# Feed-forward of a streaming encoder: up-projection in seven block products, down-projection summed in PSUM

## The chip, the core and the metric

The kernel runs on one core of a Trainium2 chip. The time is the device time of one execution in microseconds. TensorE (PE) does the matrix products into PSUM, VectorE (DVE), ScalarE (ACT) and GpSimd (POOL) the elementwise work, and SyncE (SP) issues most transfers.

## The reference

One layer of an encoder runs over a prompt of 2048 tokens and a sample of 32 (T = 2080, D = 1024). After the mixing sub-layer comes the feed-forward, which the change concerns:

```python
def conv_ffn(h, conv_state, w_up, w_dw, b_dw, w_down):
    t = h.shape[1]
    u = h @ w_up                                  # 1024 -> 2 x 2816
    uu = jnp.concatenate([conv_state.astype(u.dtype), u], axis=1)
    y = b_dw
    for j in range(CONV_W):                       # 3 taps, causal, over time
        y = y + w_dw[j] * uu[:, j:j + t]
    a, g = jnp.split(y, 2, axis=-1)
    out = (jax.nn.gelu(a, approximate=True) * g) @ w_down    # 2816 -> 1024
    return out, uu[:, -(CONV_W - 1):]
...
    h = rmsnorm(x, p['g_pre_ffn']) * (1.0 + scale_f) + shift_f
    yf, conv_new = conv_ffn(h, s_conv, p['w_up'], p['w_dw'], p['b_dw'], p['w_down'])
    x = x + gate_f * rmsnorm(yf, p['g_post_ffn'])
```

## The kernel before

Everything is kept transposed: features on the 128 partitions, tokens along the columns. Each float32 operand of a product is split into a high part (`hi`, rounded by ACT to the matmul's format) and the rest (`lo`, DVE's subtraction); `split` does that, and `mm3` makes a product of three matmuls, hi x hi, hi x lo, lo x hi.

The kernel runs through the input projection, the two mixers, and then blocks of 260 tokens (`merge`, `project`, `norms`) that merge the branches, project, normalise and write the feed-forward's input to `h2T` in DRAM. The generator `norms` of a block is advanced by `step()` while TensorE works on the next block; the last block's runs inside the feed-forward.

The feed-forward takes the tokens in six segments of 348 or 346 columns (`segs`; two more columns of the past are loaded for the conv), two segments (`si`) at a time in three passes (`sb`). `load_seg` brings a segment's eight k tiles in and splits them. For each row tile m of the 2816 (MF = 22) and each segment, `up` makes two products, the a half and the g half (`x` = 0, 1), over eight k tiles into a PSUM bank `px`; ACT and DVE apply the three conv taps, gelu and the product a*g, and split the result into an `ACT` tile. The last segment also holds the place where prompt and sample meet: `conv_outputs` copies the conv state in and the last rows out (L1397 to L1399).

`down` follows after each two row tiles: for the eight output tiles it multiplies two k tiles and adds the bank `po` to an accumulator `acc` in SBUF (L1443, L1445). After the last of them the segment's squares are summed, and `post` normalises, adds x1 and stores. Raw weights come through `wur` and `wdr` and are split by `split_up` and `split_down`, one step ahead.

The order on TensorE is that of the code. On the other engines a scheduler sets the order at build time; each then works through its queue in that order, and a waiting instruction holds those behind it. SP's queue is such a queue for the transfers.

## Time and profile before

| | us |
|---|---|
| median of 3 runs (3396.43 to 3398.52) | 3397.34 |
| the profiled execution, its own time | 3400.56 |
| its span | 3398.8 |
| PE busy | 3291.8 |
| DVE busy | 2037.2 |
| ACT busy | 1399.4 |
| POOL busy | 442.9 |

The span is the time from the first to the last instruction in the trace; the execution's own time has a few microseconds around it. The page gives the busy time of each engine with its number of instructions, then the span in 40 equal slices of about 85 us (each digit is the busy share in tenths; PEclk is TensorE's granted clock in tenths), and groups of equal instructions: line, engine, operation, output<-inputs, shapes, count, then busy time in total and mean ns of one, then idle time of the engine just before them with what ended it. In a view of windows the columns are: window, length, busy time (and count) of PE, of the weight loads, DVE, ACT and POOL, granted clock, share of the DMA engines, GB/s.

### The profile page before, as it was taken

How to read it: one execution, taken by the hardware profiler on the slowest of the kernel's cores; microseconds unless marked ns; L12 is line 12 of the kernel's file. 1: busy time of each engine (PE TensorE's matmuls, PEld its weight loads, DVE VectorE, ACT ScalarE, POOL GpSimd, SP SyncE). 2: the span in 40 equal slices, each digit the busy share in tenths (PEclk: the TensorE clock that was granted, in tenths of full speed). 3: DMA queues.
4: the chain of work that ended last, by engine and by line, in shares of the span. 5: the costliest groups of instructions: out<-in, count | busy, mean ns of one | idle time of the engine just before them, and what ended most of it. 6: DMA issues, size and time to landing. Idle time of an engine off the chain costs nothing. (4 is left out here: it accounts for less than half of the span.)

```text
span 3398.8 us, 56935 instructions
## 1 busy us (share of the span) xinstructions
PE 3291.8 (97%) x21114; PEld 3154.4 (93%) x21114; DVE 2037.2 (60%) x4837; ACT 1399.4 (41%) x3226; POOL 442.9 (13%) x593
## 2 busy tenths in 40 slices
PE   6999999999999999999999999999999999999997
PEld 5899998888999999889999999999999999999997
DVE  6735436673455555665767565557555567666666
ACT  4412224443444555544556433326433336433333
POOL 3102101111111111113544000001000001100001
PEclk8999999999999999999999999999999999999998
DMA  6434434444333334745556322224322224322211
GB/s 211 121 119 136 132 108 125 127 115 134 105 113 108 108 110 132 222 145 165 174 155 201 108 63 75 69 69 130 97 74 71 67 75 121 96 75 66 72 50 52
DMA packets 429319, 381.97 MB, mean 112 GB/s; under 512 B 40529, under 2 KB 396194, under 8 KB 429042
## 3 DMA queue, kind: packets, MB, share of 16 engines
q1 hardware_dynamic: 386082, 332.15, 33.4%
q10 hardware_dynamic: 42704, 45.93, 4.2%
q8 instruction: 166, 2.72, 0.3%
q14 instruction: 111, 0.91, 0.1%
q0 software_dynamic: 256, 0.26, 0.0%
HBM read 280.71 MB, written 97.51 MB: 111 GB/s over the span
## 5 line engine op out<-in xcount | busy, mean ns | idle before, releaser
L76 PE MATMUL px<-hA,hA 128*128 128x350 f32 (+2 forms) x2144 | 692.1, 323 | 0.0
L78 PE MATMUL px<-hA,hA 128*128 128x350 f32 (+2 forms) x2144 | 690.4, 322 | 0.0
L77 PE MATMUL px<-hA,hA 128*128 128x350 f32 (+1 forms) x2112 | 680.0, 322 | 0.0
L76 PEld LDWEIGHTS px<-hA,hA 128*128 128x128 f32 x2144 | 404.3, 189 | 0.1
L78 PEld LDWEIGHTS px<-hA,hA 128*128 128x128 f32 x2144 | 404.2, 189 | 0.0
L77 PEld LDWEIGHTS px<-hA,hA 128*128 128x128 f32 x2112 | 398.7, 189 | 0.0
L76 PE MATMUL po<-mhl,hA 128*128 128x348 f32 (+2 forms) x1184 | 372.1, 314 | 13.4 <-DVE acc L1445 7.4
L77 PE MATMUL po<-mhl,hA 128*128 128x348 f32 (+2 forms) x1184 | 369.9, 312 | 3.9 <-DVE mhl L1207 3.9
L78 PE MATMUL po<-mhl,hA 128*128 128x348 f32 (+2 forms) x1120 | 349.8, 312 | 0.0
L1445 DVE TENSOR_TENSOR acc<-acc,po 128x348 f32<-128x348 f32 (+1 forms) x480 | 242.9, 512 | 132.3 <-PE po L78 131.8
L76 PE MATMUL pm<-hA,wh 128*128 128x416 f32 x768 | 289.3, 377 | 0.0
L1418 DVE SCALAR_TENSOR_TENSOR y<-px,cw,y 128x346 f32<-128x346 f32 (+1 forms) x264 | 152.0, 576 | 215.4 <-ACT y L1417 215.2
L77 PE MATMUL pm<-hA,wh 128*128 128x416 f32 x768 | 270.4, 352 | 0.0
L78 PE MATMUL pm<-hA,wl 128*128 128x416 f32 x768 | 270.0, 352 | 0.0
L1417 ACT ACTIVATE y<-px,cw 128x346 f32<-128x346 f32 (+1 forms) x264 | 166.9, 632 | 228.1 <-PE px L78 214.0
L76 PEld LDWEIGHTS po<-mhl,hA 128*128 128x128 f32 x1184 | 224.8, 190 | 22.2 <-DVE acc L1445 12.3
L77 PEld LDWEIGHTS po<-mhl,hA 128*128 128x128 f32 x1184 | 225.5, 190 | 5.3 <-DVE mhl L1207 5.2
L70 DVE TENSOR_TENSOR hA<-wur,hA 128x1024 fp32r<-128x1024 f32 x132 | 162.8, 1234 | 101.5 <-ACT hA L67 100.0
L78 PEld LDWEIGHTS po<-mhl,hA 128*128 128x128 f32 x1120 | 213.1, 190 | 0.0
L1493 POOL TENSOR_TENSOR acc<-acc,x 128x346 f32<-128x346 f32 (+3 forms) x48 | 48.5, 1019 | 1010.0 <-DVE acc L1489 1001.2
L76 PE MATMUL pn<-wh,hA 128*128 128x256 f32 (+1 forms) x624 | 177.7, 285 | 0.0
L78 PE MATMUL pn<-wh,hA 128*128 128x256 f32 (+1 forms) x624 | 176.9, 284 | 0.0
(353 smaller groups left out, 7648.8 us busy)
## 6 DMA issues: line engine op xcount, KB each, us to landing
wur<-in_w_up_dram SPq DMA_DIRECT2D x132, 512.0 KB, 3.9
wdr<-in_w_down_dram SPq DMA_DIRECT2D x66, 512.0 KB, 4.3
wr<-in_w_in_dram SPq DMA_DIRECT2D x76, 256.0 KB, 3.5
sgT<-tx ACTq DMA_DIRECT2D x80, 208.0 KB, 2.5
wa<-in_w_ada_dram SPq DMA_DIRECT2D x64, 256.0 KB, 3.3
keys<-ks SPq DMA_DIRECT2D x128, 128.0 KB, 2.9
xk<-in_xT_dram SPq DMA_DIRECT2D x20, 416.0 KB, 4.9
tg<-sgT SPq DMA_DIRECT2D x40, 208.0 KB, 2.8
```

The costliest lines, as they stand in the source:

```text
L70: nc.vector.tensor_sub(lo, src, f32(hi))
L76: nc.tensor.matmul(out, ah, bh, start=first and i == 0, stop=False)
L77: nc.tensor.matmul(out, ah, bl, start=False, stop=False)
L78: nc.tensor.matmul(out, al, bh, start=False, stop=last and i == n - 1)
L1417: nc.scalar.activation(y[:, :o], p[:, 2:n], AF.Identity, bias=cw[:, c, 3:4], scale=cw[:, c, 2:3])
L1418: nc.vector.scalar_tensor_tensor(y[:, :o], p[:, 1:n - 1], cw[:, c, 1:2], y[:, :o], op0=OP.mult, op1=OP.add)
L1445: nc.vector.tensor_add(ac[:, m, :o], ac[:, m, :o], p[:, :o])
L1493: add.tensor_add(ac[:, m, a:e], ac[:, m, a:e], x[:, m % 2, a:e])
```

## The change

The up-projection now takes two segments together (a pair p; three pairs). The weights of a row tile are cut into four blocks, a and g half by the first and second four k tiles: A11 and A12 are the a half's, A21 and A22 the g half's. The pair's columns form B likewise (B11, B12 for the first four k tiles of the two segments, B21, B22 for the rest). Instead of eight block products there are seven, of twelve matmuls each: A11 B11, A12 B21, S1 T1, S2 T2, S3 T3, S4 B22, A22 T4, with sums S1 = A21 + A22, S2 = S1 - A11, S3 = A11 - A21, S4 = A12 - S2 of the weights and T1 to T4 of the columns.

- The column sums are made by GpSimd in `sums`, once a pair, and written to `hT` in DRAM; those of pairs 0 and 1 during the blocks of `merge` and `project`, those of pair 2 after the last block's norms, inside the feed-forward. `load_ops` reads and splits the operands of a pair, those of the next pair at the row tiles 14, 16, 18 and 21.
- The weight sums are made by GpSimd in `weights` for every row tile of every pair, into the tiles s0 to s3 (for S1 to S4; one buffer each, raw weights in `wur`). ACT makes the hi parts, DVE the lo parts, but that of A22 is GpSimd's. Split weights go round in a ring of nine places.
- `up` makes the products and joins them: p1 is A11 B11 copied out of PSUM by ACT, P5 is S1 T1, U2 is S2 T2 plus p1 and U3 is S3 T3 on top of that (both DVE). The sum of U3 and P5, the g half of the second segment, is GpSimd's (CG). DVE adds U2 to the a half of the second segment in PSUM. The g half of the first segment (`g_half`, product A22 T4) is made one row tile later, and then YG, the g half's conv, and the product with ya, the gelu. The six conv copies stand in the third pair, for both halves.
- The activations are written unsplit to `actD` in DRAM, and the accumulator, its additions, and the interleaved `down` are gone. After all three pairs the down-projection runs pair by pair and output tile by output tile over all 22 k tiles in one PSUM tile `ad` of two banks (`load_acts` brings a pair's activations back and splits them; the down weights are read again for each pair). `post` works on both segments of a pair at once.

```diff
@@ merge
-            p = psX.tile([128, 512], F32, name="px", tag=f"x{m % 2}")
+            if m % 2 == 0:
+                ad = psX.tile([128, 2, 512], F32, name="ad", tag="ad")
+            p = ad[:, m % 2]
@@ sums of the columns
+    def h_tile():
+        return fp0.tile([128, 2, W], F32, name="ht", tag="ht", bufs=3)
+    def sums(p):
+        w = WP[p]
+        for j in range(4):
+            x, y = h_tile(), h_tile()
+            load_h(x, [(0, j, 2 * p), (1, j, 2 * p + 1)], w)
+            load_h(y, [(0, 4 + j, 2 * p), (1, 4 + j, 2 * p + 1)], w)
+            yield
+            x0, x1, y0, y1 = x[:, 0, :w], x[:, 1, :w], y[:, 0, :w], y[:, 1, :w]
+            nc.gpsimd.tensor_sub(x0, x1, x0)
+            nc.gpsimd.tensor_sub(x1, y1, x1)
+            nc.gpsimd.tensor_sub(y1, y1, x0)
+            nc.gpsimd.tensor_sub(y0, y0, y1)
...
+    sumq = [(3, sums(0)), (6, sums(1)), (8, sums(2))]
@@ weights
+            for x, y in (("A11", a11), ("S2", s[1]), ("S1", s[0]), ("A12", a12), ("S3", s[2]), ("S4", s[3]), ("A22", a22)):
+                if x == "A11":
+                    nc.gpsimd.tensor_add(s[0], a21, a22)
+                    nc.gpsimd.tensor_sub(s[1], s[0], a11)
+                elif x == "S1":
+                    nc.gpsimd.tensor_sub(s[2], a11, a21)
+                    nc.gpsimd.tensor_sub(s[3], a12, s[1])
+                hi, lo = WO[p, m, x] = ring((p, m, x))
+                nc.scalar.activation(hi, y, AF.Copy)
+                sub = nc.gpsimd if x == "A22" else nc.vector
+                sub.tensor_sub(lo, y, f32(hi))
...
@@ up
+    def prod(out, p, m, x, y, first):
+        wh, wl = WO[p, m, x]
+        hi, lo = HO[p, y]
+        w = WP[p]
+        for k in range(4):
+            for i, (l_, r_) in enumerate(((wh, hi), (wh, lo), (wl, hi))):
+                nc.tensor.matmul(out[:, :w], l_[:, k], r_[:, k, :w], start=first and k == 0 and i == 0,
+                                 stop=k == 3 and i == 2, skip_group_check=True)
...
+    def conv_outputs(u, c):
+        o = TP - segs[5][0] + 2
+        nc.vector.tensor_copy(u[:, o:o + 2], stT[:, c, :])
+        nc.vector.tensor_copy(uc[:, c, 0:2], u[:, o - 2:o])
+        nc.vector.tensor_copy(uc[:, c, 2:4], u[:, o + TS:o + TS + 2])
+    def conv(y, u, c, o):
+        nc.scalar.activation(y[:, :, :o], u[:, :, 2:2 + o], AF.Identity, bias=cw[:, c, 3:4], scale=cw[:, c, 2:3])
+        for j in (1, 0):
+            nc.vector.scalar_tensor_tensor(y[:, :, :o], u[:, :, j:j + o], cw[:, c, j:j + 1], y[:, :, :o],
+                                           op0=OP.mult, op1=OP.add)
+    def g_half(p, m, b, p1, ya):
...
+        prod(b, p, m, "A22", "T4", False)
+        nc.vector.tensor_add(CG[:, 0, :w], b[:, :w], p1[:, 0, :w])
+        conv(YG, CG, m + MF, o)
+        nc.vector.tensor_mul(ya[:, :, :o], ya[:, :, :o], YG[:, :, :o])
+        nc.sync.dma_start(actD[p, m, :, :, :o], ya[:, :, :o])
+    def up(p, m, prev, side):
...
+        prod(ad[:, 0], p, m, "A11", "B11", True)
+        nc.scalar.copy(p1[:, 0, :w], ad[:, 0, :w])
+        side()
+        if prev:
+            g_half(*prev)
+        side()
+        b = psY.tile([128, 512], F32, name="po", tag="po")
+        prod(b, p, m, "S2", "T2", True)
+        nc.vector.tensor_add(U2[:, 0, :w], b[:, :w], p1[:, 0, :w])
+        side()
+        prod(ad[:, 1], p, m, "S1", "T1", True)
+        nc.scalar.copy(P5[:, 0, :w], ad[:, 1, :w])
+        side()
+        prod(ad[:, 0], p, m, "A12", "B21", False)
+        side()
+        prod(b, p, m, "S3", "T3", False)
+        nc.vector.tensor_add(U3[:, :w], b[:, :w], p1[:, 0, :w])
+        nc.gpsimd.tensor_add(CG[:, 1, :w], U3[:, :w], P5[:, 0, :w])
+        if p == 2:
+            conv_outputs(CG[:, 1], m + MF)
+        side()
+        prod(ad[:, 1], p, m, "S4", "B22", False)
+        nc.vector.tensor_add(ad[:, 1, :w], ad[:, 1, :w], U2[:, 0, :w])
+        if p == 2:
+            conv_outputs(ad[:, 1], m)
+        conv(ya, ad, m, o)
+        nc.scalar.activation(ya[:, :, :o], ya[:, :, :o], AF.Gelu_apprx_tanh)
+        side()
+        return p, m, b, p1, ya
@@ second phase
+    for p in range(3):
+        o = WP[p] - 2
+        for m in range(KD):
+            if m == KD - 1 and p < 2:
+                hq.append(load_acts(p + 1))
+            ad = psX.tile([128, 2, 512], F32, name="ad", tag="ad")
+            for k in range(MF):
...
+                for s in range(2):
+                    mm3(ad[:, s, :o], [(wh[:, k % 4], wl[:, k % 4], ah[:, s, :o], al[:, s, :o])],
+                        first=k == 0, last=k == MF - 1)
...
+            x = sq if m else sa
+            nc.scalar.activation(x[:, :, :o], ad[:, :, :o], AF.Square)
+            nc.scalar.copy(ACC[m][:, :, :o], ad[:, :, :o])
+            if m:
+                nc.vector.tensor_add(sa[:, :, :o], sa[:, :, :o], sq[:, :, :o])
+        pending.append(post(p))
```

The order on the engines at two places. First DVE's queue in the segments with the conv copies. Before, in the last pass: `px` is the PSUM bank of a product, `y` its conv, `mhl` holds split activations.

```order
L1420 SCALAR_TENSOR_TENSOR y_35742<-px,cw,y_35742 128x346
L1425 TENSOR_TENSOR y_35713<-y_35713,y_35742 128x346
L70 TENSOR_TENSOR mhl<-y_35713,mhl 128x346
L1397 COPY px<-stT 128x2
L1398 COPY uc<-px 128x2
L1399 COPY uc<-px 128x2
L1418 SCALAR_TENSOR_TENSOR y_35778<-px,cw,y_35778 128x348
```

After, in the third pair: `work` holds U2, P5, CG, YG, ya and p1, `po` and `ad` are PSUM tiles, `ring` and `hA` the places of split weights. L1464 is the split of a weight block, named by its source; L1526 makes U3, L1532 adds U2 to `ad`, L1502 is the product with ya.

```order
L1464 TENSOR_TENSOR ring_22937<-s2_29164,ring_22937 128x512
L1502 TENSOR_TENSOR work_22387<-work_22387 128x2x348
L1464 TENSOR_TENSOR ring_22937<-s3_29165,ring_22937 128x512
L1526 TENSOR_TENSOR u3_21927<-po_29190,work_22387 128x350
L1484 COPY work_22387<-stT_21923 128x2
L1485 COPY uc_21924<-work_22387 128x2
L1486 COPY uc_21924<-work_22387 128x2
L1532 TENSOR_TENSOR ad_29148<-ad_29148,work_22387 128x350
L1464 TENSOR_TENSOR ring_22937<-wur_29144,ring_22937 128x512
L1484 COPY ad_29148<-stT_21923 128x2
```

The three copies that came behind a product in PSUM now come behind a sum in SBUF, `work`, which GpSimd writes (L1527 below); the copies on `ad` come a few instructions later. The split of S4 (from s3) stands just ahead of U3.

Second, GpSimd's queue in the feed-forward. Before, between the last block's norms (`oD`, `h`) and the first `post` (`acc`), there is nothing:

```order
L1263 TENSOR_TENSOR oD<-oD,xD 128x260 x8
L1282 TENSOR_TENSOR h_22742<-oD,rstd 128x260
L1282 TENSOR_TENSOR h_22756<-oD,rstd 128x260
L1282 TENSOR_TENSOR h_22795<-oD,rstd 128x260
L1282 TENSOR_TENSOR h_22834<-oD,rstd 128x260
L1493 TENSOR_TENSOR acc_22848<-acc_22848,x_26823 128x348 x2
```

After, at the same place of the third pair as above (L1456 to L1460 are the four sums of weights, L1464 the split of A22, L1527 the sum of U3 and P5):

```order
L1460 TENSOR_TENSOR s3_29165<-wur_29010,s1_29163 128x512
L1464 TENSOR_TENSOR ring_22937<-wur_28878,ring_22937 128x512
L1527 TENSOR_TENSOR work_22387<-u3_21927,work_22387 128x350
L1456 TENSOR_TENSOR s0_29296<-wur_29146 128x512
L1457 TENSOR_TENSOR s1_29297<-s0_29296,wur_29144 128x512
L1459 TENSOR_TENSOR s2_29298<-wur_29144,wur_29146 128x512
L1460 TENSOR_TENSOR s3_29299<-wur_29144,s1_29297 128x512
L1464 TENSOR_TENSOR ring_22937<-wur_29012,ring_22937 128x512
L1527 TENSOR_TENSOR work_22387<-u3_21927,work_22387 128x350
```

Six operations per row tile are new on GpSimd, and the four sums for the next row tile (s0 to s3, of 29296 to 29299) stand ahead of the sum of U3 and P5 on which the copies above wait (the last row).

More of the change, by code (lines that the diff above doesn't have):

```diff
@@ L1296, in step @@
             queue.pop(0)
+        sum_step()
     rest = last_weights()
@@ L1519, in first, with all_weights, hstep @@
+    def all_weights():
+        yield from weights()
+        yield from down_weights()
+    wq = all_weights()
+    load_up()
+    hq = [load_ops([(0, x) for x in OPS[:4]])]
+    def hstep():
+        while hq and next(hq[0], 1) == 1:
+            hq.pop(0)
+    early = [5]
     def first():
```

488 lines of the change are left out of this document (276 added, 212 removed).

## Prediction

> **What bounds the kernel now.** I read the page first, then the windows by stage, then single rows of the feed-forward part. The page: span, busy times, and three of the forty-slice rows (TensorE, GpSimd, granted clock).
>
> ```profile
> span 3398.8 us, 56935 instructions
> PE 3291.8 (97%) x21114; PEld 3154.4 (93%) x21114; DVE 2037.2 (60%) x4837; ACT 1399.4 (41%) x3226; POOL 442.9 (13%) x593
> PE   6999999999999999999999999999999999999997
> POOL 3102101111111111113544000001000001100001
> PEclk8999999999999999999999999999999999999998
> ```
>
> TensorE is busy in every slice but the first and last; GpSimd (POOL) has next to nothing to do in the second half. The windows of that half, and the first and last matmul of the feed-forward (view of the tiles px and po):
>
> ```profile
> 1900.00:2330.00 430.00, 429.75 (x2660) 428.79 (x2660) 252.79 (x428) 145.43 (x233) 0.00 (x0) 1.00 0.25 76
> 2870.00:3340.00 470.00, 470.00 (x2935) 469.39 (x2934) 293.76 (x589) 165.90 (x255) 9.18 (x8) 1.00 0.24 72
> 3370.00:3384.00 14.00, 6.36 (x30) 4.55 (x28) 11.99 (x21) 10.48 (x24) 7.04 (x7) 0.82 0.65 183
> L77 PE MATMUL px<-hA,hA x2112: 316/321/493, 1826.8 to 3350.5; 128*128 128x350 f32 x96, 128*128 128x348 f32 x96
> L78 PE MATMUL po<-mhl,hA x1120: 277/321/493, 1542.2 to 3375.9; 128*128 128x348 f32 x72, 128*128 128x346 f32 x61, 128*128 128x260 f32 x54
> ```
>
> From 2870 to 3340 there is no gap: 2935 matmuls in 470.00 us, so one costs 0.1601 us (its row shows 0.32, because two overlap). VectorE (DVE) works 294 of the 470 us, GpSimd 9. The feed-forward is TensorE-bound; removing matmuls is worth their pitch as long as nothing else takes over. It has 6 segments x (22 x 2 x 8 x 3 + 8 x 22 x 3) = 9504 matmuls, 1521.6 us by that pitch, and runs from 1826.8 to 3376.1, 1549.3 us: 28 us of stops and slow clock. A tail of 22.7 us follows.
>
> **What is removed.** Per pair and row tile m, 2 x 48 = 96 matmuls become seven products of 12, 84: 15.37 us become 13.45. Over 66 such steps 792 matmuls go, 126.8 us. The down-projection keeps its 3168 matmuls; its 528 additions into acc go from DVE, but they were covered, so that gains nothing by itself.
>
> **What each step now asks of the other engines.** Durations come from the view by line and form:
>
> ```profile
> L1445 DVE TENSOR_TENSOR acc<-acc,po 128x348 f32<-128x348 f32 x240 | 122.0, 514 | 75.9 <-PE po L78 75.7
> L70 DVE TENSOR_TENSOR keys<-ck,keys 128x512 fp32r<-128x512 f32 x8 | 5.5, 692 | 4.4 <-ACT keys L67 4.1
> L70 DVE TENSOR_TENSOR hA<-wur,hA 128x1024 fp32r<-128x1024 f32 x132 | 162.8, 1234 | 101.5 <-ACT hA L67 100.0 <-PE po L78 1.5
> L1418 DVE SCALAR_TENSOR_TENSOR y<-px,cw,y 128x346 f32<-128x346 f32 x132 | 76.0, 576 | 140.9 <-ACT y L1417 140.8
> L1397 DVE COPY px<-stT 128x2 f32<-128x2 f32 x44 | 7.2, 164 | 24.5 <-PE px L78 24.5
> L1417 ACT ACTIVATE y<-px,cw 128x348 f32<-128x348 f32 x132 | 83.2, 630 | 81.5 <-PE px L78 67.5 <-DVE uc L1399 14.0
> L177 ACT ACTIVATE wh<-wr 128x512 fp32r<-128x512 f32 x76 | 46.9, 628 | 47.5 <-DMA wr<-in_w_in_dram 31.4 <-PE pm L77 11.8 <-ACT wh L177 2.0
> L67 ACT ACTIVATE hA<-wur 128x1024 fp32r<-128x1024 f32 x132 | 139.3, 1056 | 62.8 <-PE px L77 62.0 <-DMA wur<-in_w_up_dram 0.7
> L1282 POOL TENSOR_TENSOR h<-oD,rstd 128x260 f32<-128x260 f32 x32 | 27.4, 855 | 92.3 <-DVE rstd L149 57.8 <-DMA h2T<-h 28.5 <-ACT hA L67 2.6
> L878 POOL TENSOR_TENSOR vs<-vr,vs 128x256 fp32r<-128x256 f32 x32 | 23.8, 751 | 49.7 <-ACT vs L877 49.6
> L1263 POOL TENSOR_TENSOR oD<-oD,xD 128x260 f32<-128x260 f32 x64 | 62.7, 988 | 46.8 <-DVE oD L1261 23.8 <-DMA xD<-in_xT_dram 20.3 <-DVE sa L1269 1.8
> ```
>
> DVE and GpSimd get in each other's way. Timeline rows of both around 2348 us (start, length):
>
> ```profile
> 2347.13 0.51 DVE L1453 TENSOR_TENSOR saF<-saF,sqF 128x348 f32<-128x348 f32 x1
> 2347.56 1.25 DVE L1489 TENSOR_TENSOR acc<-acc,rstd 128x348 f32<-128x348 f32 x1
> 2348.74 0.51 DVE L1453 TENSOR_TENSOR saF<-saF,sqF 128x348 f32<-128x348 f32 x1
> 2350.32 1.36 DVE L1445 TENSOR_TENSOR acc<-acc,po 128x348 f32<-128x348 f32 x3
> 2347.29 1.15 POOL L1493 TENSOR_TENSOR acc<-acc,x 128x348 f32<-128x348 f32 x1 [0.89 <-DVE acc L1489]
> 2348.89 1.13 POOL L1493 TENSOR_TENSOR acc<-acc,x 128x348 f32<-128x348 f32 x1 [0.46 <-DVE acc L1489]
> 2350.48 0.93 POOL L1493 TENSOR_TENSOR acc<-acc,x 128x348 f32<-128x348 f32 x1 [0.46 <-DVE acc L1489]
> ```
>
> Three readings. Queued DVE operations follow at 0.43 us, 0.08 less than their length. An operation with both inputs in SBUF (0.51) waits while GpSimd reads SBUF: 1.25, ending 0.37 after GpSimd's end, so 0.14 is saved of its length. GpSimd likewise waits for such an operation and ends about 0.78 after it, instead of 0.93 alone: 0.15 saved. Operations with an input in PSUM (L1445) are not slowed.
>
> Hence, per instruction. DVE: 0.43 (350 columns), 0.61 (512), 0.81 (696, on the line from 512 to 1024), 0.87 for a multiply-add of 696; behind a GpSimd operation 0.55 for 512 and 0.81 for that multiply-add. GpSimd (line from 256 to 348): 1.25 for 512, 1.10 if it waited. ACT: 0.63 for 512, 0.92 for 696 from PSUM. One step asks of DVE 6 x 0.61 + 4 x 0.43 + 4 x 0.87 + 0.81 = 9.7 us, of GpSimd 5 x 1.25 + 0.93 = 7.2, of ACT 7 x 0.63 + 2 x 0.92 for the weights and the conv, and two copies and a gelu of less than that each, some 8.5. Each fits into 13.45. But six splits, two multiply-adds of YG and the product with ya (6.2 us of DVE) exclude GpSimd's 7.2: 13.4 us for the pair, about 1.3 less by the savings.
>
> I therefore follow one step in queue order, from the end of the split of S3. DVE's product with ya 0.81, GpSimd's s2 1.10, DVE's split of S4 0.55: 2.46. DVE adds U3 and S4's half (3.3); s3 (0.08 + 1.25) ends at 3.8; split of A11 4.35; ACT's first conv term is done at 4.3, DVE's next 5.2; GpSimd's split of A22 5.45; split of S2 6.0; 0.87, 0.43 and the split of S1 0.61 make 7.9; s0 9.25; multiply-add 10.05; s1 11.15; 0.55 + 0.87 + 0.61 bring the split of S3 at **13.2 us**. TensorE's 13.45 is longer: pairs 0 and 1 stay TensorE-bound, with 0.25 us to spare. TensorE waits only when DVE is more than some 3 us late (two products between a read of a PSUM tile and the next product into it).
>
> **The third pair** also carries the six conv copies, and the first of them waits for GpSimd's sum of U3 and P5. That sum stands in GpSimd's queue behind s3 and the split of A22, and s3 waits for the split of S4, which stands just ahead of U3 on DVE. Then: 2.46, s3 3.8, A22 5.05, the sum 6.0, three copies (0.47) 6.45, S4's add 6.9, split of A11 7.5, copy 7.65, ACT 8.6, then 0.87 + 0.61 + 0.87 + 0.43 + 0.61 = 12.0, s0 13.3, and 3.9 as above: **17.2 us**. That is 3.75 over TensorE's 13.45, in some 21 of 22 steps (the last has no next weights): **+78 us**. Bounds: 0, if GpSimd's operations are done earlier than I order them, and 100 with 0.2 us more at five handoffs.
>
> **Smaller terms.**
> - Start of the feed-forward: the last block's norms and the sums of pair 2 bring GpSimd 8 x 0.99 + 4 x 0.86 + 16 x 0.93 = 26 us and DVE about 15 us into a loop that has 0.25 us free per step. The rows below have what stops there now. I take +25, between 7 (nothing worse) and 41.
> - Sums of pairs 0 and 1 in the stage before: 32 x 0.93 = 30 us of GpSimd in stretches where it works half the time. +5 (0 to 16).
> - Operands of the next pair: 14 splits of 0.81 us each time, 11 us; 3 us are absorbed. +12 for both (0 to 22).
> - Activations return through three buffers: a load of 356 KB (about 4.2 us between the two DMA rows), ACT 0.78, DVE 0.89, 5.9 us for three, 2.0 us a tile, against TensorE's 0.96. 22 tiles take 43 us where two steps of 21.1 us are open; at the first start 14 tiles lack about 7 us. +12 (0 to 30).
> - Tail: now the statistics are ready 10.2 us after the last matmul (DVE is behind by then), the eight rows take 10 us, and the last store 2.5 (rows below). With 696 columns: squares, sum and splits 4 x 0.9, two halves of the statistics some 5, then eight rows of 0.87 + 0.2 (the sample's columns apart) with four additions of 0.81 on DVE and half of GpSimd's four of 1.6 in the way, 15, and the store: 26. +4 (0 to 8).
> - Clock, after such stops: four times 1.7 us. +7.
> - Transfers: activations out and back, and the sums out and back, are some 65 MB more over 1500 us, 43 GB/s on top of the 76 in the first window above, where the DMA engines are busy a quarter of the time. SP's queue is in order: a store of activations waits there for DVE's product, and the next raw weights stand behind it; they are needed a step later. 0 (to 10, if that step is not enough).
>
> ```profile
> PE pst L139 <- ACT sh L67: 10.2, 3, 6.1
> PE po L76 <- DVE acc L1445: 7.4, 8, 2.5
> xk<-in_xT_dram SPq DMA_DIRECT2D x20, 416.0 KB, 4.9
> sgT<-tx ACTq DMA_DIRECT2D x80, 208.0 KB, 2.5
> 3386.36 0.95 DVE L1489 TENSOR_TENSOR acc<-acc,rstd 128x348 f32<-128x348 f32 x2
> 3388.42 7.10 SPq L1496 DMA_DIRECT2D out_yT_dram<-acc  x8
> 2350.88 0.42 PE L76 MATMUL po<-mhl,hA 128*128 128x348 f32 x1 [2.54 <-DVE acc L1445]
> 2351.40:2354.80 3.40, 3.40 (x14) 3.40 (x13) 3.40 (x7) 2.30 (x5) 1.74 (x3) 0.50 0.79 246
> 1867.72 0.39 PE L139 MATMUL pst<-sh,ones 128*128 128x260 f32 x1 [1.94 <-ACT sh L67]
> 1868.00:1872.00 4.00, 3.92 (x25) 3.82 (x25) 3.69 (x7) 0.90 (x3) 0.00 (x0) 1.00 0.71 187
> ```
>
> The last four rows are the clock: after a gap of 2.54 us it was 0.50 for 3.4 us (1.7 us lost), after one of 1.94 it stayed 1.00.
>
> **Sum.** -126.8 + 78 + 25 + 5 + 12 + 12 + 4 + 7, less the 28 us of stops that the present feed-forward has: about -12. The profiled execution took 3400.6 us (span 3398.8), 3 us above the median of 3397.3, so the difference is put on the median: **3385 us**.
>
> **The rule that speaks against it.** The rows show that whichever of DVE and GpSimd waits still gets 0.14 us of its work done. The Trainium skill ("SBUF — State Buffer", section "Who interferes with whom") says that a DVE instruction with two SBUF inputs and a GpSimd instruction that reads SBUF exclude each other, and the second fully blocks. By that rule the eight savings in the walk fall away, the loop of pairs 0 and 1 is 14.3 us, and the sum 44 x 0.85 = 37 us more, 3422. The rows here differ from it and decide; it is one way into the first rival and counted there.
>
> **Rivals.**
> 1. *DVE and GpSimd bind pairs 0 and 1 too* (slower). The margin is 0.25 us in a loop of some 22 handoffs that I priced at 0.04 to 0.08 us; 0.1 us more at half of them, and the same in GpSimd's 512-column operations (1.25 is extrapolated from 348), gives 14.9. Then 44 x 1.45 = 64 us more: 3449. The gain is gone from 13.45 + 12/44 = 13.7 us a step on. For it: 16 instructions on a shared port. Against it: pieces of the rows are already contended ones.
> 2. *The third pair is not held* (faster): the sum is ready when the copies come, TensorE binds all three pairs, 3385 - 78 = 3307. For it: GpSimd's shortest operations could run under the PSUM reads; against it: s3 has one buffer and a fixed place.
> 3. *The clock falls in every step of the third pair* (slower). TensorE there waits twice for about 2 us a step (for U2 and for U3), just between the 1.94 and the 2.54 of the rows. Two drops of 3.4 us make 13.45 + 3.4 = 16.9, under 17.2: free. If a drop lasts twice as long, 20.3: 21 x 3.1 = 65 more, 3450.
>
> **Chances.** Forecast case 0.50 (its own range 3345 to 3425), rival 1 0.21, rival 2 0.20, rival 3 0.07, the rest 0.02. The forecast case lies by 0.57 below 3390.5 and by 0.16 within 0.2% (7 us, about what repeated runs tell from no change): faster 0.29 + 0.20 + 0.02, same 0.08 + 0.02, slower the rest. For eight in ten I go from rival 2 to rival 1, 3305 to 3450.
>
> **What the profile will show.** In the windows of pairs 0 and 1 TensorE near 100% and a step (22 to a pair) of 13.5 us; in the third pair steps of about 17 us, DVE waiting there for GpSimd's sum (work from u3) and TensorE for DVE; POOL above half busy in all three. DVE's splits of 512 columns near 0.9 us on average instead of 0.69. In the second phase no wait but at the three changes of pair. Wrong: steps of pairs 0 and 1 above 13.7, or of pair 2 below 15.

## The result, and the profile after

The changed kernel took 3545.8 us (median; 3542.5 to 3550.5), the kernel before 3397.9 beside it: 1.0437 times as long, 95% interval 1.0419 to 1.0455. The forecast was 3385, its range ended at 3450. The page of the changed kernel:

```profile
span 3540.4 us, 56561 instructions
PE 3229.2 (91%) x20322; PEld 3067.8 (87%) x20322; DVE 2142.0 (61%) x4525; ACT 1507.8 (43%) x3386; POOL 1038.7 (29%) x1019
PE   7999999999999999988886799989988889999896
POOL 3102101111111111123445666556654441000100
PEclk9999999999999999999997999999999999999998
```

The 792 matmuls are gone, but TensorE is busy for only 63 us less; it now stands for over a tenth of the time in 11 of the slices 18 to 33, from the merge blocks through the third pair. What it waited for from 1500 us on (us in total, times, longest):

```profile
PE ad L1478 <- ACT work L1521: 126.9, 66, 11.4
PE ad L76 <- DVE sgd L1208: 38.9, 31, 3.0
PE pst L141 <- ACT sh L67: 19.0, 2, 10.4
PE ad L77 <- DVE hA L70: 11.7, 7, 8.2
PE po L1478 <- DVE u L1526: 8.7, 1, 8.7
```

The first row is once per row tile, 66 times: a product into `ad` waits for ScalarE's copy of P5 (L1521). The second lies in the merge blocks, where L1208 is the gate operation that reads the bank. Neither is in the forecast. Three windows follow: the first seven steps, a quiet stretch of pair 0, and the third pair.

```profile
1901.00:2054.00 153.00, 108.40 (x587) 105.14 (x586) 118.22 (x151) 79.49 (x140) 93.51 (x85) 0.84 0.58 169
2090.00:2200.00 110.00, 102.78 (x627) 100.43 (x627) 103.55 (x112) 55.52 (x89) 68.07 (x46) 1.00 0.32 98
2600.00:2900.00 300.00, 258.10 (x1507) 253.01 (x1508) 220.21 (x380) 134.46 (x222) 144.51 (x111) 0.95 0.33 99
```

With 84 matmuls to a step, 627 in 110 us are 14.7 us a step (forecast 13.45; above 13.7 was its own sign of being wrong) and 1507 in 300 us are 16.7 (forecast 17.2). In the first window the clock is 0.84. Inside a step of pair 0, the matmuls that waited and ScalarE beside them (start, length; in brackets idle time and releaser):

```profile
2238.98 2.22 PE L1478 MATMUL ad<-hA,ring 128*128 128x350 f32 x12 [0.90 <-ACT work L1521]
```

```profile
2237.96 0.63 ACT L1462 ACTIVATE hA<-s 128x512 fp32r<-128x512 f32 x1 [1.12 <-PE ad L1478]
2238.50 0.43 ACT L1521 COPY work<-ad 128x350 f32<-128x350 f32 x1
```

The product that waits is A12 B21. It writes `ad[:, 0]`; the copy reads `ad[:, 1]`, where S1 T1 has just ended. The two halves are a bank each, and there is nothing in the one that the other needs; but both belong to one tile. Ahead of the copy in ScalarE's queue stands a hi part that had itself waited for TensorE.

The difference, step by step, in the spans (3540.4 less 3398.8 = 141.6; a step is the time between the first matmuls of two row tiles, excess is over 0.1601 us a matmul):

| | forecast | measured |
|---|---|---|
| matmuls removed | -126.8 | -126.8 |
| before the first product (1826.8, now 1901.4) | +5 | +74.6 |
| first seven steps, excess | +25 | +60.3 |
| rest of pairs 0 and 1, excess | 0 | +41 |
| operands at the first change of pair (two steps) | +12 for both changes | +13.5 |
| third pair, excess | +78 | +72.9 |
| second phase: 530.5 instead of 507.2 | +12 | +23.3 |
| tail: 33.2 instead of 22.7 | +4 | +10.5 |
| clock | +7 | in the rows above |
| stops of the kernel before | -28 | -28 |
| sum | -12 | +141.3 |

### The profile page after: what moved, and what is told of

It is laid out like the page before. It is cut to its first block, busy times and chain, and to the rows that moved or that the text cites. A ratio compares the mean times of both kernels' runs of the same rounds, so it can differ in the third digit from the quotient of the medians.

```text
span 3540.4 us, 56561 instructions
## 1 busy us (share of the span) xinstructions
PE 3229.2 (91%) x20322; PEld 3067.8 (87%) x20322; DVE 2142.0 (61%) x4525; ACT 1507.8 (43%) x3386; POOL 1038.7 (29%) x1019
## 5 line engine op out<-in xcount | busy, mean ns | idle before, releaser
L1478 PE MATMUL ad<-hA,ring 128*128 128x350 f32 (+1 forms) x1356 | 250.0, 337 | 66.2 <-ACT work L1521 65.6
L1478 PEld LDWEIGHTS ad<-hA,ring 128*128 128x128 f32 x1356 | 229.6, 197 | 76.8 <-ACT work L1521 75.8
L77 PE MATMUL ad<-hA,ring 128*128 128x348 f32 (+1 forms) x864 | 280.2, 324 | 11.8 <-DVE hA L70 11.7
L76 PE MATMUL ad<-hA,ring 128*128 128x348 f32 (+1 forms) x864 | 278.8, 323 | 3.8 <-ACT hA L67 3.7
L78 PE MATMUL ad<-hA,ring 128*128 128x348 f32 (+1 forms) x864 | 278.0, 322 | 0.0
L931 POOL TENSOR_SCALAR P<-P,mx 128x640 f32<-128x640 f32 (+5 forms) x136 | 101.9, 749 | 547.1 <-DVE mx L930 281.0
L77 PE MATMUL pn<-wl,hA 128*128 128x256 f32 (+1 forms) x624 | 176.7, 283 | 0.0
L77 PEld LDWEIGHTS ad<-hA,ring 128*128 128x128 f32 x864 | 163.6, 189 | 14.3 <-DVE hA L70 14.1
L1478 PE MATMUL po<-hA,ring 128*128 128x350 f32 (+1 forms) x960 | 167.2, 326 | 8.7 <-DVE u L1526 8.7
L76 PEld LDWEIGHTS ad<-hA,ring 128*128 128x128 f32 x864 | 163.6, 189 | 4.9 <-ACT hA L67 4.9
L1478 PEld LDWEIGHTS po<-hA,ring 128*128 128x128 f32 x960 | 158.0, 191 | 9.0 <-DVE u L1526 9.0
L78 PEld LDWEIGHTS ad<-hA,ring 128*128 128x128 f32 x864 | 163.4, 189 | 0.0
L1459 POOL TENSOR_TENSOR s<-wur 128x512 f32<-128x512 f32 x66 | 121.4, 1839 | 137.1 <-DVE ring L1464 78.1
L67 ACT ACTIVATE pth<-pp 128x256 fp32r<-128x256 f32 (+1 forms) x288 | 106.3, 374 | 128.2 <-PE pp L998 118.3
L1492 DVE SCALAR_TENSOR_TENSOR work<-work,cw 128x696 f32<-128x696 f32 (+1 forms) x132 | 150.5, 1140 | 9.4 <-ACT work L1490 9.2
```

What stands on the lines that cost most here:

```text
L67: i = nc.scalar.activation(hi, src, AF.Copy)
L76: nc.tensor.matmul(out, ah, bh, start=first and i == 0, stop=False)
L77: nc.tensor.matmul(out, ah, bl, start=False, stop=False)
L78: nc.tensor.matmul(out, al, bh, start=False, stop=last and i == n - 1)
L931: nc.gpsimd.tensor_scalar(P[:m, :tot], P[:m, :tot], mx[:m, 6:7], 1.0, op0=OP.mult, op1=OP.mult)
L1459: nc.gpsimd.tensor_sub(s[2], a11, a21)
```

## The experiments

All times are medians in us; the ratio is to the kernel before on the same chip, whose median beside these runs was 3395.8 to 3399.9, so a difference of a few us between two rows means nothing. "First product" is the first matmul of the feed-forward in the views' time; the expectations give it from the start of the trace, 10.5 us more. p0, p1 and p2 are the mean steps of the three pairs.

| run | us | ratio (95%) | first product | p0 | p1 | p2 |
|---|---|---|---|---|---|---|
| changed kernel | 3545.8 | 1.0437 (1.0419–1.0455) | 1901.4 | 16.94 | 15.09 | 16.76 |
| e1 | 3507.2 | 1.0319 (1.0304–1.0335) | 1869.9 | 16.90 | 15.11 | 16.78 |
| e2 | 3510.3 | 1.0325 (1.0309–1.0340) | 1901.6 | 16.23 | 14.32 | 16.51 |
| e3 | 3490.0 | 1.0264 (1.0246–1.0282) | 1900.6 | 16.12 | 13.95 | 16.22 |
| e4 | 3473.3 | 1.0220 (1.0195–1.0244) | 1859.9 | 16.24 | 14.32 | 16.54 |
| e5 (base) | 3454.9 | 1.0170 (1.0155–1.0185) | 1862.6 | 16.12 | 14.06 | 16.21 |
| e6 | 3399.8 | 1.0007 (0.9998–1.0017) | 1822.0 | 15.57 | 13.99 | 16.22 |
| e7 | 3461.2 | 1.0189 (1.0172–1.0206) | 1851.2 | 16.74 | 14.02 | 16.22 |
| e8 | 3457.5 | 1.0174 (1.0159–1.0190) | 1868.5 | 16.11 | 13.95 | 16.21 |
| e9 | 3436.4 | 1.0119 (1.0096–1.0142) | 1861.2 | 16.09 | 13.97 | 15.47 |
| e10 | 3470.5 | 1.0219 (1.0203–1.0235) | 1862.4 | 16.77 | 14.00 | 16.18 |
| e11 | 3459.9 | 1.0183 (1.0162–1.0204) | 1861.6 | 16.93 | 14.05 | 15.42 |
| e12 | 3432.3 | 1.0093 (1.0078–1.0108) | 1853.5 | 15.74 | 14.06 | 16.24 |
| e13 | 3475.4 | 1.0216 (1.0201–1.0231) | 1900.0 | 14.66 | 13.96 | 16.15 |
| e14 | 3411.0 | 1.0032 (1.0021–1.0043) | 1860.6 | 16.09 | 13.94 | 14.14 |
| e15 | 3449.7 | 1.0140 (1.0123–1.0157) | 1898.2 | 14.63 | 14.09 | 15.39 |
| e16 | 3436.8 | 1.0121 (1.0107–1.0135) | 1859.5 | 15.98 | 13.98 | 15.75 |
| e17 | 3424.7 | 1.0085 (1.0070–1.0099) | 1836.2 | 16.32 | 14.00 | 15.75 |
| e18 | 3401.6 | 1.0007 (0.9994–1.0019) | 1839.9 | 16.58 | 14.06 | 14.31 |

### The two-bank tile: e1 to e5

e1 changes the merge alone:

```diff
-            if m % 2 == 0:
-                ad = psX.tile([128, 2, 512], F32, name="ad", tag="ad")
-            p = ad[:, m % 2]
+            p = psM.tile([128, 512], F32, name="px", tag=f"x{m % 2}")
```

> Only the merge blocks get their four one-bank tiles back (closed before the feed-forward). Theory A (a two-bank PSUM tile holds the next product until the other half is read): the waits of TensorE on the merge's gate operation, 39 us in the changed kernel, go, with their slow clock and what they held up; the first matmul of the feed-forward comes at 1835 to 1870 instead of 1912, and the time falls from 3545.8 to 3480 (3465 to 3505). Rival B (GpSimd's sums of the columns, which run in the same blocks, hold the merge): the first matmul stays above 1895 and the time at 3530 to 3546. Rival C (the delay is real but only moves into the start of the feed-forward, where the last norms and the sums of pair 2 are late anyway): the first matmul comes early, the first seven steps take as much longer, the time stays at 3530 to 3546.

The time is 38.7 us less, and the first product comes 31.5 us earlier. That is theory A in kind, though both lie a little above its ranges. The row on `sgd` is gone; what stays in the waits from 1500 us to the first product is

```profile
PE pst L141 <- ACT sh L67: 16.5, 2, 10.4
PE po L76 <- ACT sqD L1242: 8.9, 2, 5.1
PE po L76 <- ACT sa L1239: 8.6, 2, 8.2
```

The first product still comes 43 us later than before the change.

e2 changes the order of two products:

```diff
+        prod(ad[:, 0], p, m, "A12", "B21", False)
+        side()
         prod(ad[:, 1], p, m, "S1", "T1", True)
         nc.scalar.copy(P5[:, 0, :w], ad[:, 1, :w])
         side()
-        prod(ad[:, 0], p, m, "A12", "B21", False)
-        side()
```

> Only TensorE's order changes: the product A12 B21 stands ahead of S1 T1, so a product of 1.9 us that needs nothing of ScalarE's P5 copy... stands on the other side of it. Theory A (A12 waits for the P5 copy, because both are in one tile): the wait in front of A12 goes, steps of pairs 0 and 1 fall from 14.65 to 13.5 us (44 x 1.15 = 51 us), the third pair from 16.8 to 16 to 16.8; time 3485 (3465 to 3500). Rival D (VectorE and GpSimd on their shared port bind the loop at 14.6 us; the wait is only where TensorE meets it): steps stay at 14.4 to 14.7, TensorE waits elsewhere, on VectorE; time 3535 to 3550.

The time is 35.5 us less, short of theory A's range. The quiet steps are 13.8 us, so most of the wait goes. What is left is put down to VectorE, which is 98% busy here: TensorE's weight loads wait for it up to 0.4 us a step (window, then wait, both of e2):

```profile
2090.00:2200.00 110.00, 109.76 (x669) 107.41 (x668) 107.95 (x120) 57.98 (x96) 74.57 (x50) 1.00 0.33 102
```

```profile
PEld po L1478 <- DVE u L1526: 2.6, 8, 0.4
```

e3 leaves the order and takes the tile apart:

```diff
-        ad = psX.tile([128, 2, 512], F32, name="ad", tag="ad")
+        ad = [psU.tile([128, 512], F32, name="px", tag=f"x{x}") for x in range(2)]
...
-        conv(ya, ad, m, o)
+        for x in range(2):
+            conv(ya[:, x:x + 1], ad[x].rearrange("p (x w) -> p x w", x=1), m, o)
```

> The up-projection's two-bank tile becomes two one-bank tiles, the order of products is unchanged; the conv of the a half is done per segment (two more ScalarE and two more VectorE operations a step, about 0.3 us of each). Theory A (the wait is taken per tile): A12 no longer waits for the P5 copy, steps of pairs 0 and 1 fall to 13.5 to 13.9 us; time 3490 (3470 to 3510). Rival E (A12 waits for something that ScalarE makes, its queue being late, not for the tile): the wait in front of A12 stays, steps 14.6 to 15, time 3545 to 3565. Rival D (VectorE and GpSimd bind): steps 14.6 to 15 too, but TensorE waits on VectorE.

The time is 55.8 us less, although three operations a step were added (the expectation says four). The same window as above, in e3:

```profile
2090.00:2200.00 110.00, 110.00 (x686) 110.00 (x685) 103.69 (x139) 64.54 (x106) 74.70 (x49) 1.00 0.35 107
```

686 matmuls in 110 us: 13.47 us a step, TensorE without a gap and VectorE at 94%. So the wait that made 14.7 us of a step was the tile's, not ScalarE's lateness (rival E) nor VectorE's and GpSimd's exclusion (rival D).

> The merge's one-bank tiles and A12 ahead of S1 together. Theory A: both gains add, 3545.8 - 65 - 60 = 3420 (3400 to 3450), still slower than the kernel before by the third pair, by the start of the feed-forward and by the down weights. If the parts only exchange waits (rivals C and D), 3500 or more.

The gains in e4 add (72.5 us against 38.7 + 35.5), but I had set their sum at 125. e5 joins e1 and e3 and is the base of the rest:

> One-bank tiles in the merge and in the up-projection together (the edits of the first and the third run; this is the base of the next three). Theory A: the gains of the two, 38.7 and 55.8 us, add: 3545.8 - 94.5 = 3451 (3440 to 3465); first matmul of the feed-forward at 1870 to 1882, steps of pairs 0 and 1 at 13.5 us, of the third pair at 16.2. If the merge's gain is taken back in the first seven steps, 3475 or more.

The time is 3454.9, 90.9 us less than the changed kernel: the two gains add to within 4 us. What is left against the kernel before is 56 us.

### The column sums: e6, e7, e12, e17

e6 loads the operands T straight from `h2T` and sets `sumq = []`.

> On that base, the column sums T1 to T4 are left out: the operands are loaded straight from the feed-forward's input (the same loads, no sums, no store and return). It prices all that the sums do to the other work. Theory S (what is left of the 43 us before the feed-forward, and most of the 57 us of the first eight steps, is the sums: their loads, GpSimd's operations and their stores stand in queues ahead of the merge's and of the raw weights): first matmul at 1825 to 1840, first eight steps together 165 down to 115 to 135 us; time 3375 (3360 to 3395). Rival F (the start is late for its own reasons, the last norms and the first raw weights, which come as late without the sums): first matmul at 1855 to 1880, first steps as long, time 3430 to 3455.

The time is 55.1 us less and level with the kernel before: 40.6 us of it lie before the first product, 12 in pair 0. Theory S holds for the blocks before the feed-forward; in the loop rival F has the larger part, since the first eight steps still take 153 us, and the time is 5 us above theory S's range. One way in which the sums reach TensorE is seen in the base: SyncE's queue, then ScalarE's row, then the waits of TensorE.

```profile
1814.69 4.03 SPq L1340 DMA_DIRECT2D hT<-ht  x2
1818.83 0.41 SPq L1442 DMA_DIRECT2D wur<-in_w_up_dram  x1
1819.33 1.18 SPq L1316 DMA_DIRECT2D ht<-h2T  x2
1820.56 0.42 SPq L1442 DMA_DIRECT2D wur<-in_w_up_dram  x1
```

```profile
1824.36 1.15 ACT L1461 ACTIVATE hA<-wur 128x512 fp32r<-128x512 f32 x2 [6.53 <-DMA wur<-in_w_up_dram]
```

```profile
PE pst L141 <- ACT sh L67: 15.5, 2, 10.1
PE po L76 <- ACT sa L1239: 8.4, 2, 8.0
PE po L76 <- ACT sqD L1242: 7.9, 2, 4.2
```

A store of sums holds SyncE's queue for 4 us, until GpSimd has made them; the first raw weights stand behind it, ScalarE waits 6.5 us for them at the head of its queue, and behind that stands the copy out of PSUM (L1239) that frees TensorE's bank: 8.0 us. Without the sums those rows read

```profile
PE po L76 <- ACT sa L1239: 4.6, 1, 4.6
PE pst L141 <- ACT sh L67: 0.8, 1, 0.8
```

e7 issues the stores from GpSimd (`nc.gpsimd.dma_start`).

> On the base, only the stores of the column sums are issued by GpSimd instead of SyncE, so that SyncE's queue no longer stands still until GpSimd has made a sum (two stores took 3.8, 2.1, 2.7, 2.2, 4.0, 2.5 and 2.7 us of SyncE's queue in the stretch 1687 to 1838 of the run with both edits). Theory S1 (SyncE's queue in order is what passes the delay on: gates of the merge, norms and raw weights stand behind the store): first matmul of the feed-forward at 1835 to 1860, time 3425 (3405 to 3440). Rival S2 (GpSimd's own time is what counts, its sums stand ahead of the norms' additions in its queue): first matmul unchanged within 8 us, time 3443 to 3460; issuing costs GpSimd something, so it may be slower.

The first product came 11 us earlier, outside both expectations, and pair 0 took 14 us more. The median is 6 us above the base, but the intervals of the two overlap. e12 keeps loads and stores and drops the four `tensor_sub`.

> On the base with one-bank tiles, the column sums keep their loads and stores, but GpSimd's four subtractions per block of rows are left out. The first matmul of the feed-forward came at 1873 us in the base and at 1832.5 without any sums. Theory P (GpSimd's operations, ahead of the merge's and the norms' additions in its queue and on the port that it shares with VectorE, cost those 40 us): first matmul at 1834 to 1848, time 3405 to 3425. Rival Q (SyncE's queue and the transfers: loads and stores that wait for a free buffer stand ahead of gates, norms and raw weights): first matmul at 1858 to 1873, time 3435 to 3455.

The first product came only 9 us earlier, as by rival Q; the time, 3432.3, is just under that rival's range. So of the 40 us some 9 are GpSimd's arithmetic and some 31 come with the loads and stores. The place shown above belongs to the arithmetic, for which the store waits there: in e12 the row on L1239 is gone. What holds TensorE longest in e12, 12.8 us, is the statistics of the last block. Ahead of them GpSimd's queue is held by transfers. An addition of the norms (L1266) waits 6.22 us for its input; then the zeroing of two columns of a buffer (L1313) waits 5.51 us until a store of sums has landed, and the last addition stands behind it:

```profile
PE pst L141 <- ACT sh L67: 16.0, 2, 12.8
```

```profile
1840.20 0.73 POOL L1266 TENSOR_TENSOR oD<-oD,xD 128x260 f32<-128x260 f32 x1 [6.22 <-DMA xD<-in_xT_dram]
1846.44 0.13 POOL L1313 MEMSET ht<- 128x2 f32 x2 [5.51 <-DMA hT<-ht]
1846.53 0.73 POOL L1266 TENSOR_TENSOR oD<-oD,xD 128x260 f32<-128x260 f32 x1
```

How the 31 us divide between SyncE's queue, GpSimd's queue and the transfers' own time is not shown. e17 (on e16, below) spreads the sums:

```diff
-    sumq = [(3, sums(0)), (6, sums(1)), (8, sums(2))]
+    sumq = [(3, sums(0)), (8, sums(1)), (8, sums(2))]
...
+        turn[0] += 1
+        if turn[0] % 3 == 0 or ndone[0] >= 8:
+            sum_step()
```

> As the run before, and the column sums of pair 0 advance at every third place of the merge blocks instead of at every one; those of pair 1 start after the last norms, inside the feed-forward, like those of pair 2. If bunching in SyncE's queue is what the sums cost the merge blocks (31 of the 40 us), the first matmul of the feed-forward comes at 1840 to 1852 instead of 1873, the loop of pair 0 takes 10 to 18 us more for pair 1's sums, and the time is 15 us (5 to 25) under that of the run before, 3396, level with the kernel before. Rival: spread out they hold the blocks as much, or the loop gives back all of it: no change or up to 10 us slower.

The first product came 23 us earlier than in e16, 7.5 us were given back in pair 0, and the time is 12 us less, as expected in kind. But the edit does two things: it spreads the sums of pair 0 and takes those of pair 1 out of these blocks. If the two pairs cost alike, half of the 40.6 us would go with pair 1's sums alone, so what the spreading adds is not shown.

### The first steps: e10, e13

Here the last block's norms are moved. e10 calls `step()` at two of the seven places of a row tile.

> On the base, the last block's norms, and then the sums of pair 2, advance at two places of each step of pair 0 instead of at all seven. Theory N (the first eight steps take 165 us instead of 108 because the norms' VectorE and GpSimd operations come all at once on engines that have next to nothing free): spread out they fit, the first fifteen steps take 30 us less, time 3425 (3410 to 3440). Rival O (the first steps are late for the operands of pair 0 and the first weights, which are read and split there in any case): the first three steps stay at 25, 24 and 15 us, time 3445 to 3460. Rival W (the work is the same and the loop has no room for it at any pace): the same sum over 22 steps, 3450 to 3460.

The kernel is 15.5 us slower, which is rival W and more. Spread over 14 steps the norms cost 14 us more than bunched in eight; at neither pace does the loop have room for them. e13 finishes the norms first (`while queue: step()` ahead of the loop).

> On the base, the last block's norms are carried out before the first product of the feed-forward, TensorE waiting; the sums of pair 2 stay in the loop. The first product comes some 20 us later, at 1885 to 1900. Theory N2 (the norms' operations are what fills VectorE and GpSimd in the first steps): the first eight take 120 to 135 us instead of 163, time 3430 to 3450. Rival O (they are late for pair 0's operands and the first weights): the first eight steps stay above 150 us, time 3460 to 3480.

The first eight steps took 133 us instead of 166, as theory N2 has it, so the norms are 32 of their 60 us of excess. But the first product came 37 us later, not 20, and the second phase took 17 us longer (waits on activations 22 instead of 11 us), so that the time is rival O's; why the second phase is longer I did not settle. e15 has this edit together with e9's (below):

> The sum of U3 and P5 on VectorE in the third pair, and the norms ahead of the first product, on the base: 3436 less what the norms' place brings, 3415 to 3430 if theory N2 holds, 3440 to 3460 by rival O. Still above the kernel before (3398) in either case, since the column sums before the feed-forward stay.

The time is 3449.7, rival O's number, though the first eight steps take 133 us here too: the first product is as late as in e13.

### The third pair: e8, e9, e14, e16, e18

e8 moves the three copies on the g half.

> On the base, the three copies on the g half of the third pair are written down one row tile's product later, next to the conv that reads them, so VectorE no longer meets GpSimd's sum of U3 and P5 just ahead of U2's addition. Theory T (the third pair's 16.2 us a step come from VectorE waiting for that sum): steps of the third pair fall to 13.5 to 14 us, time 3451 - 22 x 2.4 = 3398 (3390 to 3410). Rival (six more VectorE operations and the shared port bind there anyway, the wait is a symptom): steps stay above 15.3, time above 3430.

e8 wrote the copies down later, but the scheduler put them back: VectorE's queue was that of e5 but for one copy in one step. It is a repeat of e5 (2.5 us apart) and tells nothing. In both, VectorE does the following in each such step (rows of e5):

```profile
2712.78 0.17 DVE L1483 COPY work<-stT 128x2 f32<-128x2 f32 x1 [3.05 <-POOL work L1526]
2728.79 0.17 DVE L1483 COPY work<-stT 128x2 f32<-128x2 f32 x1 [3.05 <-POOL work L1526]
```

It stands 3.05 us for GpSimd's sum, as the forecast's walk said, and comes back to it 16.0 us later. e9 gives that sum to VectorE in the third pair:

```diff
-        nc.gpsimd.tensor_add(CG[:, 1, :w], U3[:, :w], P5[:, 0, :w])
+        (nc.vector if p == 2 else nc.gpsimd).tensor_add(CG[:, 1, :w], U3[:, :w], P5[:, 0, :w])
```

> On the base with one-bank tiles, in the third pair alone the sum of U3 and P5 is VectorE's instead of GpSimd's, straight behind U3 in its queue. (The run with the late copies left VectorE's queue as it was but for two rows, so it tested nothing: the scheduler put the copies back to the same place.) Theory T (VectorE stands for some 3 us a step until GpSimd's sum is done, and TensorE behind it for U2): steps of the third pair fall from 16.2 to 13.5 to 14.3 us, time 3455 - 45 = 3410 (3395 to 3422). Rival (VectorE's six copies and GpSimd's sums of weights hold the third pair anyway): steps stay above 15.3, time above 3435.

The time is 18.5 us less, at the rival's end of the two forecasts, and the later steps are 15.2 us. The wait for the sum is gone, and VectorE is the busiest engine, 221 of 240 us; it is the one that TensorE waits for. The sum and the first copy behind it each take longer than their own 0.5 and 0.2 us, while GpSimd is at work (its row beside the copy is in the last section):

```profile
2600.00:2840.00 240.00, 217.64 (x1331) 213.22 (x1331) 220.71 (x380) 114.72 (x202) 119.45 (x79) 1.00 0.30 90
```

```profile
2727.67 1.22 DVE L1526 TENSOR_TENSOR work<-u,work 128x350 f32<-128x350 f32 x1
2728.93 1.14 DVE L1483 COPY work<-stT 128x2 f32<-128x2 f32 x1
2729.98 0.16 DVE L1484 COPY uc<-work 128x2 f32<-128x2 f32 x1
```

e11 joins e9 and e10.

> Both edits together on the base. If both theories hold, 3455 - 45 - 30 = 3380 (3365 to 3400), level with the kernel before or under it. What would be left over the forecast then lies before the feed-forward (40 us from the column sums), in the first steps, and in the second phase.

With both edits the time is 3459.9, where the two effects alone would give 3452; the paced norms cost more, not less, here too. e14 leaves the copies out (but for one step):

> On the base, the six conv copies of the third pair are left out in all steps but the first (the sample's columns are not joined to their state, so that the outputs of the sample and of the conv state are not the reference's). Theory T2 (the copies, and what waits behind them, are the whole difference between the third pair and the others; the sum on GpSimd then stands in nobody's way): steps of the third pair 13.5 us instead of 16.2, time 3455 - 55 = 3400 (3392 to 3410). Rival (something else of the third pair holds it): steps above 14.5, time above 3420.

The time is 44 us less, and the steps are 13.5 us from the fifth on. The copies, with what waits behind them, are the whole difference between the third pair and the others. e16 gives them to ScalarE (`nc.scalar.copy`):

> On the base with one-bank tiles, the six conv copies of the third pair are ScalarE's, in whose queue the conv that reads them follows. If only their place in VectorE's queue was wrong (the theory: VectorE stands until GpSimd's sum is done, and TensorE behind it), steps of the third pair fall from 16.2 to 13.5 to 14.1 us and the time to 3411 (3405 to 3425), as without any copies. Rival: ScalarE stands for GpSimd's sum instead, and the weights' hi parts and the copy of P5 stand behind it: steps 15 us or more, time above 3435.

This is the rival: ScalarE stands instead, 5.86 us a step, and VectorE behind it. A step is 15.4 us.

```profile
2731.79 0.19 ACT L1483 COPY work<-stT 128x2 f32<-128x2 f32 x1 [5.86 <-POOL work L1526]
```

e18 puts the three copies on the g half behind the sum in GpSimd's own queue and has e17's order of sums:

```diff
+            conv_outputs(CG[:, 1], m + MF, nc.gpsimd.tensor_copy)
```

> As e17, but the three copies on the g half stand behind the sum of U3 and P5 in GpSimd's own queue (those on the a half stay with ScalarE, ahead of its conv). Theory (the place in the queue is the cost: no engine on TensorE's path waits for GpSimd's sum any more): steps of the third pair 13.5 to 13.8 us, as without copies, and 3425 - 22 x 1.8 = 3385 (3378 to 3398), level with the kernel before or just under it. Rival (the copies' own time, and GpSimd's three more operations on the shared port, cost as much): steps above 14.8, time above 3412.

```profile
2600.00:2800.00 200.00, 198.83 (x1217) 194.98 (x1216) 190.72 (x244) 115.44 (x231) 134.87 (x128) 1.00 0.33 101
```

1217 matmuls in 200 us are 13.8 us a step, the top of the theory's range, with the six copies still made. The time, 3401.6 us, is 4 us above the theory's range and no different from the kernel before. No version beat that kernel.

## Why the prediction was wrong

The steps that failed are two waits that were put at nothing (a tile of two banks, in the loop and in the merge) and two terms that were too small (the sums before the feed-forward, and its start).

**What bounds the kernel, and the pitch: right.** There are 792 matmuls fewer at 0.1601 us, and where nothing stops TensorE a step is 13.47 us (e3).

**"Pairs 0 and 1 stay TensorE-bound": wrong as the kernel stood.** The walk through one step priced VectorE's and GpSimd's queues, but no wait of TensorE on ScalarE. "TensorE waits only when DVE is more than some 3 us late" was said of readers of the bank that is written next; the build holds a product for the reader of the tile's other half too. The price is 1.2 us a step, 41 us in the table and 55.8 by e3, which has the third pair in it. The walk's margin (VectorE done at 13.2 of 13.45) was not there either: with the forecast's own operations and the wait mostly gone, e2's step is 13.8 us and VectorE 98% busy. That is the first rival in small, 13.8 and not 14.9. With the conv cut by segment (e3) VectorE is 94% busy and TensorE binds. The Trainium skill ("SBUF — State Buffer", sections "Who interferes with whom" and "Summary: rules for kernel authors") has the second instruction block fully, which made the loop 14.3 us. Neither e2 nor e3 comes to that, and the changed kernel has the saving again: a split of 0.68 us that met a sum of GpSimd ended 0.55 us after it.

```profile
2236.78 1.92 POOL L1457 TENSOR_TENSOR s<-s,wur 128x512 f32<-128x512 f32 x1
2237.47 1.78 DVE L1464 TENSOR_TENSOR hA<-wur,hA 128x512 fp32r<-128x512 f32 x1
2240.02 0.68 DVE L1464 TENSOR_TENSOR hA<-s,hA 128x512 fp32r<-128x512 f32 x1
```

**The merge's tile: costed at nothing, without a word.** The diff's first lines put two row tiles of the merge into one two-bank tile; the sum has no term for it and names no cover. It cost 38.7 us (e1). The Trainium skill ("PSUM — Partial Sum Buffer", section "PSUM bank collisions raise a hardware error") asks that accesses of two engines be kept apart by bank and quadrant; between the halves of `ad` that asks for no wait, and e1 and e3, where the same accesses run without one, agree.

**"Sums of pairs 0 and 1 in the stage before", +5 (0 to 16): mis-sized, 40.6 by e6.** I counted GpSimd's 30 us and what they displace (9 us by e12), not their loads and stores, 31 us. The bullet on transfers has SyncE's order, but for the activations' store alone and at 0 (to 10). By the rows of e5 and e12 both SyncE's and GpSimd's queue are held; moving the stores out of SyncE's queue (e7) brought the first product 11 us forward.

**"Start of the feed-forward", +25 (7 to 41): mis-sized, 60.3.** The operations were listed, but set against 0.25 us of free time per step as if they cost their length beyond it. Of the 153 us TensorE idled 44.6; its 587 matmuls took 108.4 busy us instead of 94, so some 14 us go to the slow clock (0.84 in this window), twice the whole clock term. By the runs the norms are about 32 (e13) and the sums some 12 (e6); operands and first weights were not tried apart.

**The third pair, +78: the wait that it names is there; the nearness of 72.9 is partly luck.** In the third pair of the changed kernel (2606 to 2977) VectorE waits for GpSimd's sum in 21 steps, but TensorE, which the forecast has waiting for VectorE, waits for ScalarE's copy and the tile in all 22:

```profile
DVE work L1484 <- POOL work L1527: 57.8, 21, 3.2
PE ad L1478 <- ACT work L1521: 51.5, 22, 4.2
```

With the tile apart a step is 16.2 us, where 17.2 was forecast: 61 us over TensorE's 13.45 in 22 steps. So some 12 of the 72.9 us are the tile's again. The second rival (not held) fell. The third (a fall of the clock that costs nothing more) is seen at its edge: waits up to 2.6 us and a mean clock of 0.97 in the base, up to 2.3 us and 1.00 in e16. In the base TensorE's steps go from 14.5 to 17.5 us while VectorE's wait comes every 16.0 us, so there the falls cost nothing.

```profile
2600.00:2860.00 260.00, 231.46 (x1370) 226.83 (x1370) 191.09 (x378) 119.58 (x211) 132.25 (x97) 0.97 0.28 85
2600.00:2840.00 240.00, 214.85 (x1315) 210.51 (x1315) 174.09 (x264) 118.86 (x289) 128.82 (x95) 1.00 0.29 90
```

```profile
PE po L1477 <- DVE work L1517: 37.0, 22, 2.6
```

```profile
PE po L1477 <- DVE work L1517: 31.7, 19, 2.3
```

In each pair of rows the base stands first (the second pair are waits of the third pair).

**Return of the activations, +12, and tail, +4: 23.3 and 10.5.** The first is within its bounds (0 to 30), the second just beyond (0 to 8); neither was taken apart. **Operands at a change of pair:** 13.5 at the first change, against 12 for both.

So the size of the miss, 153 us, is 70 before the feed-forward, 41 in the quiet steps of pairs 0 and 1, 35 in the first steps, 18 in the second phase and tail, less 11 in what was set too high or counted apart. The range missed first because all its cases took the build's waits as those of the data. Without them (e5) the time is 3454.9, still 5 us above the end of the range, mostly through the two mis-sized terms.

## What to carry to other kernels

Look first at what a change does to PSUM tiles: in this build a product waited for the reader of the tile's other half, so halves that different engines read at different times belong in tiles of their own. When work is moved into another stage, price its loads and stores, and what stands behind them in every queue that issues them or waits for their buffers, not its arithmetic alone. Small operations that must wait for a slow engine's result did best here in that engine's own queue, behind what they wait for (e18).

## What the runs showed of the hardware

A VectorE copy of two columns within SBUF, one input only, took 1.14 us in e9 (its row stands above, from 2728.93) while GpSimd's split was under way, and ended 0.03 us after that; free of it, the copy took 0.17 us (e5).

```profile
2728.47 1.57 POOL L1463 TENSOR_TENSOR hA<-wur,hA 128x512 fp32r<-128x512 f32 x1
```

I had taken only operations with two inputs in SBUF to wait. The same copy on ScalarE took 0.19 us (e16), where GpSimd was idle beside it.
